# A dense layer on quarter products: sums made in the output projection, and the down product on 7 of 8 quarter products too

## The chip, the core and the metric

One core of a Trainium2 chip runs the program alone. The metric is the device time of one execution, in microseconds (us), as the median over runs. Per core there are the matrix engine (PE), the vector engine (DVE), the activation engine (ACT), GpSimd (POOL), and the sync engine (SP), which here issues loads; 16 DMA engines move data between HBM (also the kernel's own scratch tensors) and on-chip memory (SBUF). PE writes to accumulators (PSUM).

## The reference, cut to what matters

A decoder trunk of two layers on 1024 rows of width 1024, all in fp32. The change lies in the first layer's second half and at its borders:

```python
def swiglu(h, w_gate, w_up, w_down):
    return (jax.nn.silu(h @ w_gate) * (h @ w_up)) @ w_down
...
h = h + retnet_gla_mixer(hn, positions, ab_w_in[e], ..., ab_w_out[e])
h = h + swiglu(rms_norm(h, norm_ffn_g[l]), ffn_w_gate[e], ffn_w_up[e], ffn_w_down[e])
```

The hidden width is 2816 = 22 tiles of 128. The second layer (an HGRN2 mixer, then routed experts) follows.

## The kernel before, in words

**Three matmuls for one.** Each fp32 operand is held as two fp32r numbers, hi and lo; `mm3` (L154 to L156) does hi x hi, lo x hi and hi x lo. ACT makes hi by a copy and DVE makes lo by a subtraction: `whi`, `wlo` for weights (L142, L143, or `split_to`, L817, L818), `xhi`, `xlo` for activations. Two raw weight tiles ("wst") and four split ones fit in the weight pool.

**Order.** The program is written as one stream; a scheduler of the framework gives each engine its own list, and every engine works through its list in order. An instruction that waits holds all behind it on its engine, also a load on SP or a store on POOL. `defer` puts off a piece of work by some `tick`s of the program. A tile from a pool with n buffers waits until the last reader of the tile n allocations ago is done.

**Output projection** (`outproj`, `outproj_ab`). For each of 8 row tiles: load h, two accumulations of 24 matmuls, two adds on DVE (L765), then store h to scratch, norm to hn (ACT L192, POOL L182 and L184, DVE L194), and by `rows_to_fm` turn hn with 8 transposes on PE (L204) into the two halves of x (`xhi`, `xlo`: 8 blocks of features by 512 rows).

**Gate and up** (`gate_up_quads`). The two products gate and up are taken as one 2x2 block product: rows in two halves, features in two halves, and [gate, up] as two columns. Seven products of quarters (Winograd's form of Strassen's scheme) replace eight. `quad_sums` makes four sums of quarters of x on DVE (L833, L838), and splits them, while the first tile runs. For each f of 22, `quad_weights` loads the gate and up weights of one tile (512 KB each, into "raw", 8 buffers), makes four sums on DVE (L880 to L883) and splits all; then seven products of 12 matmuls follow in accumulators A, B, C and Dk, with copies on ACT (p1, p5, d, u2) and adds on DVE between. The sixth product adds to C, so it waits for C's copy p5 (L914). Two 256 KB stores of hid per f go through POOL's queue (L922, L928).

**Down** (`ffn_down`). Row tiles in groups of 3, 3 and 2. For each group, hid is read from scratch two f tiles at a time (L956) and split, w_down is loaded whole, and 1056 matmuls in all add up over 22 tiles; then h is added (L973), stored, normed and turned for the next mixer, `mix_c`.

Of the kernel before, what the change touches and what calls it, by code (L numbers as in the profile page):

```python
# [18 lines left out]
T = 1024  # L19
# [21 lines left out]
FFN_TILES = ((0, 3), (3, 3), (6, 2))  # L41
# [33 lines left out]
class Trunk:  # L75
# [142 lines left out]
    def build(self, upto=9):  # L218
        nc, tc = self.nc, self.tc
        with ExitStack() as ctx:  # L220
# [8 lines left out]
            with self.pool("hnp") as self.hnp:  # L229
# [3 lines left out]
                with self.pool("op") as self.op, self.pool("w2") as w2:  # L233
                    x = self.outproj_ab(oT, (w2, 0, 4))
                if upto < 2:
                    return
                pc = self.ffn(x)
# [511 lines left out]
    def outproj(self, w, src, oT, w2, pairs, done):  # L749
# [8 lines left out]
        for t in range(8):  # L758
            h = self.t(self.op, [P, D], "h", 6)
# [9 lines left out]
    def outproj_ab(self, oT, w2):  # L769

        nc = self.nc
        g = self.gain_rows(self.op, "gain", self.i["norm_ffn_g"][0])
        x = [None, None]

        def place(hn, t):
            if t % 4 == 0:
                x[t // 4] = self.half()
            self.rows_to_fm(self.dn, hn, x[t // 4], t % 4)

        def done(h, t):  # L780
            nc.gpsimd.dma_start(self.s["h0"][t * P:(t + 1) * P, :], h)
            hn = self.norm_rows(self.op, "hn", h, g)

            self.defer(max(1, 4 * (t // 4) + 3 - t), place, hn, t)

        self.outproj(self.i["ab_w_out"][0], self.i["x"][0], oT, w2, (0, 2, 3, 1), done)
        self.flush()
        return x
# [21 lines left out]
    def ffn(self, x):  # L810

        with self.pool("ffs") as fs:
            self.gate_up_quads(fs, x)
        return self.ffn_down(x)

    def split_to(self, hi, lo, src):
        self.nc.scalar.activation(hi, src, AF.Copy)  # L817
        self.nc.vector.tensor_tensor(lo, src, hi.bitcast(F32), op=OP.subtract)  # L818

    def quad_sums(self, fs, x):  # L820


        tt = self.nc.vector.tensor_tensor
        quarter = [[[a[:, 4 * c:4 * c + 4, :] for a in x[r]] for c in range(2)] for r in range(2)]

        def tiles():
            return [self.t(fs, [P, 2, HT], "raw", 8) for _ in range(2)]

        def whole(q):
            out = tiles()  # L830
            for n, o in enumerate(out):
                hi, lo = (a[:, 2 * n:2 * n + 2, :].bitcast(F32) for a in q)
                tt(o, hi, lo, op=OP.add)  # L833
            return out

        def sums(dst, a, b, op):
            for o, p, q in zip(dst, a, b):
                tt(o, p, q, op=op)  # L838
            return dst

        def split(src, name):
            s = [self.t(fs, [P, 4, HT], name + n, 1, F32R) for n in ("hi", "lo")]
            for n, r in enumerate(src):
                self.split_to(*(a[:, 2 * n:2 * n + 2, :] for a in s), r)
            return s
# [673 lines left out]
```

## Time and profile before

| | us |
|---|---|
| median of three runs | 4001.97 (4001.89 to 4003.94) |
| profiled execution, its own time | 4004.72 |
| its span in the trace | 4003.0 |
| gate/up: first to last matmul | 566.62 to 1006.58 |
| down: first to last matmul | 1022.01 to 1270.61 |

A row of the timeline gives start, length, engine, line, operation, result <- operands, a count, and in brackets how long the engine had been idle and what it had waited for. Matmul rows overlap: a 128x512 one has 0.39 us, but at full clock the next starts 0.23 later, so spacing is what counts. PEclk is the granted clock of PE as a share of the higher of its two levels, 2.4 GHz; 0.5 is the lower, 1.2 GHz.

### The profile page before, as it was taken

The page shows a single profiled execution, that of the slowest core. Times are in us where ns is not written, and L with a number is a line of the kernel's source. Part 1 is how long each engine was busy: PE and PEld are TensorE (multiplying, and loading weights), DVE is VectorE, ACT ScalarE, POOL GpSimd, SP SyncE. Part 2 cuts the span into 40 slices and gives each one's busy share as a digit, 9 for nine tenths or more (in the row PEclk, how much of TensorE's full clock was granted, in tenths as well). Part 3 has the DMA queues.
Part 4 walks back from the last instruction along what each step waited for, and adds up shares of the span by engine and source line. Part 5 has one row for each costly group of instructions (what it writes and reads, how often), then busy time and mean ns, then how long its engine had stood idle before and what let it go on. Part 6 is the DMA issues. An engine that isn't in the chain of part 4 may idle for free. (4 is left out here: it accounts for less than half of the span.)

```text
span 4003.0 us, 63918 instructions
## 1 busy us (share of the span) xinstructions
PE 3886.5 (97%) x26096; PEld 3600.8 (90%) x26096; DVE 2037.9 (51%) x2974; ACT 1500.0 (37%) x2311; POOL 278.6 (7%) x418
## 2 busy tenths in 40 slices
PE   8999989999899999999799999999999999999998
PEld 7888868888688889998798999999999999999996
DVE  5743356554355363354554544544545545455564
ACT  4212323333344222222344444444434444444453
POOL 1011000000001000003100000000000000000012
PEclk9999989999999999999899999999999999999999
DMA  4011313221665111113466555555555555566686
GB/s 133 27 48 61 127 51 99 82 82 63 193 201 182 43 33 53 43 64 123 161 192 201 165 175 176 164 160 192 183 171 179 184 184 182 189 190 201 211 287 223
DMA packets 436559, 568.17 MB, mean 142 GB/s; under 512 B 25734, under 2 KB 340390, under 8 KB 436256
## 3 DMA queue, kind: packets, MB, share of 16 engines
q1 hardware_dynamic: 415120, 493.87, 38.5%
q0 software_dynamic: 21136, 70.13, 5.0%
q8 instruction: 206, 3.38, 0.4%
q14 instruction: 97, 0.79, 0.1%
HBM read 511.11 MB, written 51.87 MB: 141 GB/s over the span
## 5 line engine op out<-in xcount | busy, mean ns | idle before, releaser
L143 DVE TENSOR_TENSOR wlo<-wst,whi 128x1024 fp32r<-128x1024 f32 (+1 forms) x816 | 995.7, 1223 | 1285.4 <-ACT whi L142 1272.3
L142 ACT ACTIVATE whi<-wst 128x1024 fp32r<-128x1024 f32 (+1 forms) x816 | 859.5, 1056 | 1097.9 <-PE pj L155 588.0
L155 PE MATMUL pj<-mxl,whi 128*128 128x256 f32 (+5 forms) x3584 | 1028.7, 287 | 0.2 <-DVE mxl L1242 0.2
L156 PE MATMUL pj<-mxh,wlo 128*128 128x256 f32 (+5 forms) x3584 | 1028.2, 287 | 0.0
L154 PE MATMUL pj<-mxh,whi 128*128 128x256 f32 (+5 forms) x3584 | 1026.9, 287 | 0.1
L154 PEld LDWEIGHTS pj<-mxh,whi 128*128 128x128 f32 x3584 | 675.5, 188 | 0.7 <-ACT sl L1259 0.3
L155 PEld LDWEIGHTS pj<-mxl,whi 128*128 128x128 f32 x3584 | 675.2, 188 | 0.5 <-DVE mxl L1242 0.4
L156 PEld LDWEIGHTS pj<-mxh,wlo 128*128 128x128 f32 x3584 | 673.4, 188 | 0.0
L154 PE MATMUL pj<-whi,xhi 128*128 128x256 f32 (+2 forms) x1280 | 400.9, 314 | 6.0 <-DVE h L973 4.0
L155 PE MATMUL pj<-wlo,xhi 128*128 128x256 f32 (+2 forms) x1280 | 398.9, 312 | 0.3 <-DVE wlo L143 0.3
L156 PE MATMUL pj<-whi,xlo 128*128 128x256 f32 (+2 forms) x1280 | 398.9, 312 | 0.0
L154 PE MATMUL dn<-mhh,whi 128*128 128x288 f32 (+4 forms) x1120 | 326.2, 291 | 0.0
L155 PE MATMUL dn<-mhl,whi 128*128 128x288 f32 (+4 forms) x1120 | 325.3, 290 | 0.0
L156 PE MATMUL dn<-mhh,wlo 128*128 128x288 f32 (+4 forms) x1120 | 325.1, 290 | 0.0
L154 PEld LDWEIGHTS pj<-whi,xhi 128*128 128x128 f32 x1280 | 248.8, 195 | 18.6 <-issue 4.8
L155 PEld LDWEIGHTS pj<-wlo,xhi 128*128 128x128 f32 x1280 | 249.4, 195 | 9.9 <-DVE wlo L143 1.0
L156 PEld LDWEIGHTS pj<-whi,xlo 128*128 128x128 f32 x1280 | 249.1, 195 | 9.3
L154 PE MATMUL pj<-xhi,whi 128*128 128x512 f32 x624 | 246.2, 395 | 5.4 <-ACT whi L817 3.5
L156 PE MATMUL pj<-xhi,wlo 128*128 128x512 f32 x624 | 245.5, 393 | 0.1
L155 PE MATMUL pj<-xlo,whi 128*128 128x512 f32 x624 | 244.8, 392 | 0.0
L155 PEld LDWEIGHTS dn<-mhl,whi 128*128 128x128 f32 x1120 | 210.9, 188 | 0.0
L156 PEld LDWEIGHTS dn<-mhh,wlo 128*128 128x128 f32 x1120 | 210.7, 188 | 0.0
(359 smaller groups left out, 5449.8 us busy)
## 6 DMA issues: line engine op xcount, KB each, us to landing
wst<-in_moe_w_gate_dram SPq DMA_DIRECT2D x224, 512.0 KB, 3.8
wst<-in_moe_w_up_dram SPq DMA_DIRECT2D x224, 512.0 KB, 3.9
wst<-in_moe_w_down_dram SPq DMA_DIRECT2D x224, 512.0 KB, 4.4
wst<-in_ffn_w_down_dram SPq DMA_DIRECT2D x66, 512.0 KB, 3.6
wst<-in_c_w_in_dram SPq DMA_DIRECT2D x32, 512.0 KB, 3.7
wst<-in_ab_w_in_dram SPq DMA_DIRECT2D x26, 512.0 KB, 3.8
scr_h<-h POOLq DMA_DIRECT2D x24, 512.0 KB, 3.4
raw<-in_ffn_w_gate_dram SPq DMA_DIRECT2D x22, 512.0 KB, 3.8
```

Source lines behind the costliest of these rows:

```text
L142: act = nc.scalar.activation(hi, st, AF.Copy)
L143: dve = nc.vector.tensor_tensor(lo, st, hi.bitcast(F32), op=OP.subtract)
L154: mm(ps, l[0], r[0], start=start, stop=False, **kw)
L155: mm(ps, l[0], r[1], start=False, stop=False, **kw)
L156: self.last_mm = mm(ps, l[1], r[0], start=False, stop=stop, **kw)
```

## The change

The turned quarters of x and their four sums are no longer made from xhi and xlo in front of gate/up, but from rows of hn in the output projection: hn of row tiles 0 to 3 is stored to scratch, and for tiles 4 to 7 the matching tile of the upper half is loaded again (`ht`), three sums of rows are made on POOL (on DVE for the last tile), and everything is turned by `turn`. The fourth sum is kept as rows in scratch (`s3r`) and turned at the start of gate/up. The f tiles are taken in pairs (j, j + 11), third and fourth product change places. After each pair POOL makes four sums of its hid blocks and stores seven blocks, and four sums of w_down's quarters (1 MB, `wd`, one buffer), stored to scratch `wt`. The down product then is seven quarter products of 132 matmuls over all rows, 924 in all, accumulated into h; h is loaded up front.

```diff
-    def quad_sums(self, fs, x):
...
+    def turn(self, rows, dst, t):
+        ps = self.dn([P, 4, P])
+        for k in range(4):
+            self.nc.tensor.transpose(ps[:, k, :], rows[:, k * P:(k + 1) * P], self.ident)
+        self.split_to(*(a[:, :, t * P:(t + 1) * P] for a in dst), ps)
...
         def done(h, t):
             nc.gpsimd.dma_start(self.s["h0"][t * P:(t + 1) * P, :], h)
             hn = self.norm_rows(self.op, "hn", h, g)
+            if t < 4:
+                nc.gpsimd.dma_start(self.s["hn0"][t * P:(t + 1) * P, :], hn)
+                self.defer(1, place, hn, t)
+                return
+            ht = self.t(self.op, [P, D], "ht", 1)
+            r = slice((t - 4) * P, (t - 3) * P)
+            nc.sync.dma_start(ht, self.s["hn0"][r, :])
+            s1 = h[:, L]
+            tt = (nc.vector if t == 7 else nc.gpsimd).tensor_tensor
+            tt(s1, hn[:, L], hn[:, R], op=OP.add)
+            tt(hn[:, L], ht[:, L], hn[:, L], op=OP.subtract)
+            tt(ht[:, L], s1, ht[:, L], op=OP.subtract)
+            tt(ht[:, R], ht[:, R], ht[:, L], op=OP.subtract)
+            nc.gpsimd.dma_start(self.s["s3r"][r, :], hn[:, L])
+            self.defer(1, place2, hn, t - 4, ht, s1)
...
-        g, u = (self.t(fs, [P, 2, 4, P], "raw", 8) for _ in range(2))
+        g, u = (self.t(wp, [P, 2, 4, P], "wst", 2) for _ in range(2))
...
-        ta, tb = (self.t(fs, [P, 2, 4, P], "raw", 8) for _ in range(2))
+        ta, tb = (self.t(fs, [P, 2, 4, P], "raw", 4) for _ in range(2))
...
+            for f in [a * NH + j for j in range(NH) for a in range(2)]:
+                W = self.quad_weights(fs, wg, wu, f * P)
+                if f == 0:
+                    for t in range(4):
+                        r = sn()
+                        nc.sync.dma_start(r, self.s["s3r"][t * P:(t + 1) * P, :])
+                        self.turn(r, X[6], t)
...
+                    self.keep("hid", 3, j, a22)
+                    pt(s1, a21, a22, op=OP.add)
+                    self.keep("hid", 4, j, s1)
+                    pt(a21, a11, a21, op=OP.subtract)
...
+                    b = self.t(fs, [P, 2, 2, HT], "wd", 1)
+                    nc.sync.dma_start(b, wd.rearrange("(r p) (c n) -> p r c n", p=P, c=2)[:, j::NH])
+                    pt(b[:, 0, 0], b[:, 0, 1], b[:, 0, 0], op=OP.subtract)
+                    pt(b[:, 0, 1], b[:, 1, 1], b[:, 0, 1], op=OP.subtract)
+                    pt(b[:, 1, 1], b[:, 1, 1], b[:, 0, 0], op=OP.subtract)
+                    pt(b[:, 1, 0], b[:, 1, 1], b[:, 1, 0], op=OP.subtract)
+                    for n, a in enumerate((b[:, 0, 0], b[:, 1, 1], b[:, 0, 1], b[:, 1, 0])):
+                        self.keep("wt", n, j, a)
...
+        W = [wd[:, :NH, :HT], wd[:, NH:, :HT], wd[:, NH:, HT:], wt[3], wt[0], wt[1], wt[2]]
...
+            hs = [self.t(fp, [P, D], "h", 8) for _ in range(8)]
+            for t, h in enumerate(hs):
+                nc.sync.dma_start(h, self.s["h0"][t * P:(t + 1) * P, :])
...
+            def product(n, ps, first=True, last=True):
...
+                    own = n or j0
+                    for dst, src, pool in ((l, hv[n], fp if own else None), (r, W[n], None)):
+                        wp = self.wps[0][0]
+                        st = self.t(pool or wp, [P, 2, HT], "wst", 4 if pool else 2)[:, :nj]
+                        nc.sync.dma_start(st, src[:, js])
+                        dst += [self.t(pool or wp, [P, 2, HT], a, 3 if pool else 4, F32R)[:, :nj] for a in ("whi", "wlo")]
+                        self.split_to(*dst, st)
+                    for j in range(nj):
+                        for u in range(4):
+                            self.mm3(ps[u], [a[:, j, u * P:(u + 1) * P] for a in l], [a[:, j, :] for a in r],
+                                     first and j0 + j == 0, j0 + j == NH - 1, **kw)
...
+            product(2, B, False)
+            add(0, 1, B)
+            for t in range(4):
+                self.defer(1 + t, finish, t)
+            A = [self.pj([P, HT]) for _ in range(4)]
+            product(3, A)
+            pc = self.piece(i["c_w_in"][0], 2048)
+            self.flush()
+            add(1, 0, A, OP.subtract)
+            for t in range(4, 8):
+                finish(t)
```

The change moves instructions in three places. PE, at the end of the output projection, before: from its last matmul to the first of gate/up (pj600).

```order
L156 MATMUL pj556_4608<-whi503_4092,xlo435_3806 128x512
L204 MATMUL dn562_4644<-ident_64,hn545_4511 128x128 x4
L204 MATMUL dn563_4651<-ident_64,hn545_4511 128x128 x4
L204 MATMUL dn564_4658<-ident_64,hn551_4573 128x128 x4
L204 MATMUL dn565_4665<-ident_64,hn551_4573 128x128 x4
L204 MATMUL dn566_4672<-ident_64,hn557_4635 128x128 x4
L204 MATMUL dn567_4679<-ident_64,hn557_4635 128x128 x4
L204 MATMUL dn571_4694<-ident_64,hn568_4687 128x128 x4
L204 MATMUL dn572_4701<-ident_64,hn568_4687 128x128 x4
L154 MATMUL pj600_4785<-xhi529_4390,whi578_4719 128x512
L155 MATMUL pj600_4785<-xlo530_4391,whi578_4719 128x512
L156 MATMUL pj600_4785<-xhi529_4390,wlo579_4720 128x512
```
And after, from the last turn of row tile 6 on (pj609, the first product, with 12 matmuls, stands just ahead; hn578, h563 and ht581 are row tile 7, sn601 to sn607 the four s3r rows; dn610 is the second product):

```order
L782 MATMUL dn577_4749<-ident_64,ht573_4721 128x128 x4
L782 MATMUL dn582_4771<-ident_64,hn578_4757 128x128 x4
L782 MATMUL dn583_4778<-ident_64,h563_4631 128x128 x4
L782 MATMUL dn584_4785<-ident_64,ht581_4764 128x128 x4
L782 MATMUL dn585_4792<-ident_64,ht581_4764 128x128 x4
L782 MATMUL dn602_4834<-ident_64,sn601_4832 128x128 x4
L782 MATMUL dn604_4843<-ident_64,sn603_4841 128x128 x4
L782 MATMUL dn606_4852<-ident_64,sn605_4850 128x128 x4
L153 MATMUL pj611_4870<-s0hi479_4043,whi595_4820 128x512
L154 MATMUL pj611_4870<-s0lo480_4044,whi595_4820 128x512
L782 MATMUL dn608_4861<-ident_64,sn607_4859 128x128 x4
L153 MATMUL dn610_4869<-xhi432_3803,whi593_4812 128x512
```
Transposes of tiles that come from scratch (ht, sn) now stand among the first matmuls of gate/up, and the second product stands behind the last of them.

SP, in the first f tiles of gate/up, before (574 and 575 are the weights of the first f tile, and so on):

```order
L868 DMA raw574_4713<-in_ffn_w_gate_dram 128x8x128
L868 DMA raw575_4714<-in_ffn_w_up_dram 128x8x128
L868 DMA raw608_4891<-in_ffn_w_gate_dram 128x8x128
L868 DMA raw609_4892<-in_ffn_w_up_dram 128x8x128
L868 DMA raw628_5023<-in_ffn_w_gate_dram 128x8x128
L868 DMA raw629_5024<-in_ffn_w_up_dram 128x8x128
L868 DMA raw648_5155<-in_ffn_w_gate_dram 128x8x128
L868 DMA raw649_5156<-in_ffn_w_up_dram 128x8x128
```
And after, from behind the loads of s3r (617 and 618 are the second f tile's):

```order
L938 DMA wd638_5114<-in_ffn_w_down_dram 128x2x1024
L852 DMA wst617_4972<-in_ffn_w_gate_dram 128x8x128
L852 DMA wst618_4973<-in_ffn_w_up_dram 128x8x128
L852 DMA wst639_5124<-in_ffn_w_gate_dram 128x8x128
L938 DMA wd680_5396<-in_ffn_w_down_dram 128x2x1024
L852 DMA wst640_5125<-in_ffn_w_up_dram 128x8x128
L938 DMA wd722_5678<-in_ffn_w_down_dram 128x2x1024
L852 DMA wst659_5254<-in_ffn_w_gate_dram 128x8x128
L938 DMA wd764_5960<-in_ffn_w_down_dram 128x2x1024
L852 DMA wst660_5255<-in_ffn_w_up_dram 128x8x128
L852 DMA wst681_5406<-in_ffn_w_gate_dram 128x8x128
L938 DMA wd806_6242<-in_ffn_w_down_dram 128x2x1024
```
Between the weights of the f tiles now stand the loads of w_down's quarters, three for two f tiles; there are eleven.

ACT, in the middle of an f tile, before (sn646 is p5, the copy of accumulator C, pj642; raw648 and raw650 are weights and a sum of weights of the f tile after):

```order
L817 ACTIVATE whi652_5161<-raw648_5155 128x1024
L912 ACTIVATE sn644_5053<-sn644_5053 128x512
L914 ACTIVATE sn646_5055<-pj642_5051 128x512
L817 ACTIVATE whi654_5169<-raw650_5159 128x1024
L916 ACTIVATE sn645_5054<-dn643_5052 128x512
L918 ACTIVATE sn647_5056<-pj640_5049 128x512
```
And after (sn657 is p5, the copy of C, pj653; wst659 and raw661 belong to the f tile after):

```order
L775 ACTIVATE whi663_5260<-wst659_5254 128x1024
L903 ACTIVATE sn655_5154<-sn655_5154 128x512
L905 ACTIVATE sn656_5155<-dn654_5153 128x512
L775 ACTIVATE whi665_5268<-raw661_5258 128x1024
L907 ACTIVATE sn657_5156<-pj653_5152 128x512
L909 ACTIVATE sn658_5157<-pj651_5150 128x512
```
The split of the next f tile's first sum (raw661, made on DVE from its gate and up weights) has moved from behind p5 to ahead of it.

SP, at the border to the down product, before:

```order
L132 DMA wst1060_7795<-in_ffn_w_down_dram 128x1024
L132 DMA wst1063_7819<-in_ffn_w_down_dram 128x1024
L214 DMA gain1029_7667<-in_norm_mix_g_dram 128x1024
L951 DMA h1030_7669<-scr_h0 128x1024
L951 DMA h1031_7671<-scr_h0 128x1024
L951 DMA h1032_7673<-scr_h0 128x1024
L956 DMA hid1039_7681<-scr_hid 128x2x384
L956 DMA hid1048_7735<-scr_hid 128x2x384
L956 DMA hid1057_7789<-scr_hid 128x2x384
```
And after (wst1073, the hid rows of the first two tiles of the first product, was loaded before these; wst1079 are those of the next two):

```order
L986 DMA wst1106_8157<-in_ffn_w_down_dram 128x512
L986 DMA wst1116_8189<-in_ffn_w_down_dram 128x2x512
L213 DMA gain1060_7949<-in_norm_mix_g_dram 128x1024
L966 DMA h1061_7951<-scr_h0 128x1024
L966 DMA h1062_7952<-scr_h0 128x1024
L966 DMA h1063_7953<-scr_h0 128x1024
L966 DMA h1064_7954<-scr_h0 128x1024
L966 DMA h1065_7955<-scr_h0 128x1024
L966 DMA h1066_7956<-scr_h0 128x1024
L966 DMA h1067_7957<-scr_h0 128x1024
L966 DMA h1068_7958<-scr_h0 128x1024
L986 DMA wst1079_8007<-scr_hid 128x2x512
```
Eight loads of h now stand where three stood, and the second load of hid stands behind all of them.

## Rows read from the trace of the kernel before

**Rows 1.** The page's first part: busy time, share of the span, instructions.

```profile
PE 3886.5 (97%) x26096; PEld 3600.8 (90%) x26096; DVE 2037.9 (51%) x2974; ACT 1500.0 (37%) x2311; POOL 278.6 (7%) x418
```
**Rows 2.** Windows: busy time of each engine with its count of instructions, then granted clock of PE, share of DMA time, GB/s. Two parts of gate/up, the middle of the stop behind it, and down.

```profile
566.60:612.00 45.40, 34.76 (x108) 24.62 (x108) 41.76 (x44) 16.39 (x20) 1.16 (x2) 0.80 0.19 58
612.00:1008.00 396.00, 394.73 (x1740) 326.53 (x1740) 219.76 (x290) 153.67 (x212) 22.16 (x41) 1.00 0.25 81
1014.00:1022.00 8.00, 0.00 (x0) 0.00 (x0) 0.01 (x1) 0.84 (x1) 0.00 (x0) 0.50 1.02 396
1030.00:1270.00 240.00, 239.83 (x1081) 198.26 (x1080) 122.93 (x124) 99.18 (x118) 13.18 (x18) 1.00 0.61 194
```
**Rows 3.** Timeline, the end of the output projection and the start of gate/up.

```profile
555.28 0.40 PE L156 MATMUL pj<-whi,xlo 128*128 128x512 f32 x1
555.52 3.27 PE L204 MATMUL dn<-ident,hn 128*128 128x128 f32 x24
555.72 0.69 DVE L765 TENSOR_TENSOR h<-h,pj 128x512 f32<-128x512 f32 x1 [4.76 <-PE pj L156]
561.63 1.94 PE L204 MATMUL dn<-ident,hn 128*128 128x128 f32 x8 [2.84 <-DVE hn L194]
566.62 0.80 PE L154 MATMUL pj<-xhi,whi 128*128 128x512 f32 x1 [3.06 <-ACT whi L817]
```
**Rows 4.** Timeline, the last matmuls of gate/up and the start of down.

```profile
1004.54 0.39 PE L156 MATMUL pj<-s3hi,wlo 128*128 128x512 f32 x1
...
1006.58 0.39 PE L156 MATMUL pj<-s3hi,wlo 128*128 128x512 f32 x1
1009.34 0.68 DVE L927 TENSOR_TENSOR sn<-sn,sn 128x512 f32<-128x512 f32 x1
1010.31 1.62 SPq L951 DMA_DIRECT2D h<-scr_h  x3
1012.02 1.78 SPq L956 DMA_DIRECT2D hid<-scr_hid  x3
1021.12 0.84 ACT L817 ACTIVATE hh<-hid 128x768 fp32r<-128x768 f32 x1 [12.76 <-DMA hid<-scr_hid]
1022.01 0.79 PE L154 MATMUL pj<-whi,hh 128*128 128x512 f32 x1 [15.04 <-ACT hh L817]
```
**Rows 5.** Timeline, matmuls of down after that stop.

```profile
1026.58 0.63 PE L155 MATMUL pj<-wlo,hh 128*128 128x512 f32 x1
1027.01 0.63 PE L156 MATMUL pj<-whi,hl 128*128 128x512 f32 x1
...
1028.29 0.44 PE L156 MATMUL dn<-whi,hl 128*128 128x512 f32 x1
1028.57 0.39 PE L154 MATMUL dn<-whi,hh 128*128 128x512 f32 x1
```
**Rows 6.** Groups of instructions by line and shape, 540 to 1280 us: shape, count, busy us, mean ns of one, idle time before them.

```profile
L818 DVE TENSOR_TENSOR wlo<-raw,whi 128x1024 fp32r<-128x1024 f32 x66 | 80.5, 1223 | 86.5 <-ACT whi L817 86.5
L817 ACT ACTIVATE whi<-raw 128x1024 fp32r<-128x1024 f32 x66 | 69.7, 1060 | 116.7 <-PE dn L155 74.1 <-PE pj L155 35.2 <-PE pj L156 4.5
L881 DVE TENSOR_TENSOR raw<-raw,raw 128x512 f32<-128x512 f32 x22 | 15.0, 684 | 0.0
L914 ACT ACTIVATE sn<-pj 128x512 f32<-128x512 f32 x22 | 13.2, 598 | 33.0 <-PE pj L156 33.0
L922 POOL DMA_DIRECT2D scr_hid<-sn x22 | 12.0, 544 | 349.2 <-DVE sn L921 349.2
```
**Rows 7.** DMA issues: count, KB each, median us from issue to landing.

```profile
raw<-in_ffn_w_gate_dram SPq DMA_DIRECT2D x22, 512.0 KB, 3.8
wst<-in_ffn_w_down_dram SPq DMA_DIRECT2D x66, 512.0 KB, 3.6
scr_hid<-sn POOLq DMA_DIRECT2D x44, 256.0 KB, 2.3
hid<-scr_hid SPq DMA_DIRECT2D x11, 256.0 KB, 3.6
```
**Rows 8.** POOL beside DVE: a group by line, then the timeline at three places far from the change.

```profile
L623 POOL TENSOR_TENSOR qq<-qq,t 128x512 f32<-128x512 f32 x8 | 12.4, 1549 | 20.5 <-DVE t L622 20.2
L623 POOL TENSOR_TENSOR qk<-qk,t 128x512 f32<-128x512 f32 x8 | 10.2, 1279 | 31.2 <-DVE t L622 30.9
260.56 1.23 DVE L143 TENSOR_TENSOR wlo<-wst,whi 128x1024 fp32r<-128x1024 f32 x1
260.61 2.33 POOL L623 TENSOR_TENSOR qq<-qq,t 128x512 f32<-128x512 f32 x1 [0.83 <-DVE t L622]
18.34 1.27 DVE L194 SCALAR_TENSOR_TENSOR s<-qk,rstd,vg 128x1024 f32<-128x1024 f32 x1
29.27 0.66 POOL L289 CAST mk<-row 128x576 uint8<-128x576 f32 x1
29.35 1.66 DVE L194 SCALAR_TENSOR_TENSOR s<-qk,rstd,vg 128x1024 f32<-128x1024 f32 x1 [0.29 <-POOL rstd L184]
```
**Rows 9.** Timeline, the end of down and the first matmul of mix_c.

```profile
1270.61 0.39 PE L156 MATMUL pj<-whi,hl 128*128 128x512 f32 x1
1275.03 0.55 PE L154 MATMUL pj<-whi,xhi 128*128 128x256 f32 x1 [4.03 <-DVE h L973]
```

More of the change, by code (lines that the diff above doesn't have):

```diff
@@ L40 @@
 EPS = 1e-6
-FFN_TILES = ((0, 3), (3, 3), (6, 2))
 LEVELS = (1, 2, 4, 8, 16, 32, 64)
@@ L232, in build @@
                     oT = self.mix_ab(x)
[L233 to L237, printed above, removed]
+                x = [None, None]
+                with self.pool("fs") as fs:
+                    X = [[self.t(fs, [P, 4, HT], f"s{n}{a}", 1, F32R) for a in ("hi", "lo")] for n in range(2)]
+                    with self.pool("op") as self.op, self.pool("w2") as w2:
+                        self.outproj_ab(oT, (w2, 0, 4), X)
+                    if upto < 2:
+                        return
+                    q = [[[a[:, 4 * c:4 * c + 4, :] for a in oT[r]] for c in range(2)] for r in range(2)]
+                    self.ffn_gate_up([q[0][0], q[0][1], q[1][0], q[1][1], X[0], X[1], None])
+                pc = self.ffn_down(x)
                 if upto < 3:
@@ L746, in mix_c, with outproj @@
         return oT
-    def outproj(self, w, src, oT, w2, pairs, done):
+    def outproj(self, w, src, oT, w2, pairs, done, nh=6):
         nc = self.nc
@@ new lines, in product @@
+            def product(n, ps, first=True, last=True):
+                kw = {} if first else dict(skip_group_check=True)
+                for j0 in range(0, NH, 2):
+                    nj = min(2, NH - j0)
+                    js = slice(j0, j0 + nj)
+                    l, r = [], []
+                    own = n or j0
+                    for dst, src, pool in ((l, hv[n], fp if own else None), (r, W[n], None)):
+                        wp = self.wps[0][0]
+                        st = self.t(pool or wp, [P, 2, HT], "wst", 4 if pool else 2)[:, :nj]
[6 more added lines that the diff above has]
+                                     first and j0 + j == 0, j0 + j == NH - 1, **kw)
+                    self.tick()
@@ new lines, in add @@
+            def add(r, c, ps, op=OP.add):
+                for u in range(4):
+                    hc = hs[4 * r + u][:, c * HT:(c + 1) * HT]
+                    tt(hc, hc, ps[u], op=op)
+            A = [self.pj([P, HT]) for _ in range(4)]
+            product(0, A)
+            add(0, 0, A)
+            B = [self.dn([P, HT]) for _ in range(4)]
+            product(1, B)
+            add(0, 0, B)
+            product(5, A, False)
+            add(0, 1, A)
+            B = [self.dn([P, HT]) for _ in range(4)]
@@ L976, in ffn_down @@
+            product(4, B)
+            add(1, 1, B)
+            product(6, A, False)
+            add(1, 0, A)
+            add(1, 1, A)
+            product(2, B, False)
+            add(0, 1, B)
+            for t in range(4):
+                self.defer(1 + t, finish, t)
+            A = [self.pj([P, HT]) for _ in range(4)]
+            product(3, A)
+            pc = self.piece(i["c_w_in"][0], 2048)
             self.flush()
+            add(1, 0, A, OP.subtract)
+            for t in range(4, 8):
+                finish(t)
```

189 lines of the change are left out of this document (72 added, 117 removed).

## The prediction

> **What bounds the kernel now.** I read the page's first part (PE busy 97% of the span [rows 1]: time is saved only by giving PE less, or by closing a stop), then the windows over the dense layer [rows 2], then the timeline at its three borders [rows 3, 4, 9]. In 612 to 1008 us PE is busy 394.73 of 396 us at full clock, and DVE, ACT and DMA have room: PE's matmuls set that stage. Before it, in 566.6 to 612, PE has 34.76 of 45.4 us at a mean clock of 0.80. Behind it lies a stop of 15 us, which ends on the load of hid [rows 4], and behind the second product one of 4 us [rows 9]. One 128x512 matmul costs (1006.58 - 1004.54) / 9 = 0.2267 us. All offsets below count from the last output-projection add, 555.72 [rows 3]. Gate/up ends at 1006.81, which is +451.1; its 22 x 7 x 12 = 1848 matmuls need 418.9, so 21.3 of its 440.2 us are stops and half clock, nearly all ahead of 612.
>
> **Output projection.** Four rows of sums are turned there too: 16 more transposes at 3.27/24 = 0.136 us [rows 3], **+2.2**. The loads of hn, its stores and POOL's sums lie beside its matmuls, until the last tile.
>
> **The front of gate/up.** The sums on DVE and the 11.3 us between the last output-projection matmul and the first of gate/up go. What is late next is a chain through DRAM: PE runs in order, and the turns of the last two tiles and of the s3r rows stand ahead of the second product. There is one ht buffer. Its tile for t=5 is turned by +2; load 3.8 [rows 7]; three POOL sums that need it, 1.28 each [rows 8]; eight transposes, +10.8; the next load 3.8, one DVE sum 0.69, POOL's issue 0.54 [rows 6] and the store's 2.3, then a 256 KB load at 3.6 [rows 7]: **+22**. By then 14 of the 1848 matmuls are done. The other 1834 take 415.8 and the restart costs 3 us of half clock (14 matmuls at 0.43 in place of 0.23, as after the stop of down [rows 5]). Without other stops gate/up ends at +440.8: **-10.3**. Bounds: 4 us either way, by the loads.
>
> **The new chain in gate/up.** The rows of w_down are summed on POOL while gate/up runs. They have one buffer, so a load waits for the four stores of the load before, and SP, in order, holds the up-weights behind it: after the fourth wd load comes the fourth tile's up-weights, and so on, three wd loads for two tiles, until the eleventh. A cycle is: the 1 MB load, 3.8 plus 512 KB more at 396 GB/s (1.33) [rows 2, 7] = 5.1; four POOL sums; four issues 4 x 0.54; the last store's 2.3. For a POOL sum the rows give 1.28 alone, 2.33 beside a DVE instruction with both inputs in SBUF; I take 1.55, the mean of the eight of qq [rows 8], since DVE is busy 219.76 of 396 us [rows 2]. Cycle: 5.1 + 6.2 + 2.2 + 2.3 = 15.8. Each pair of tiles adds its own four sums and seven stores, 6.2 + 3.8 = 10 us of POOL, about half of it under a wd load: 5. So the chain needs 3 x 15.8 + 5 = 52.4 us for what PE does in 168 x 0.2267 = 38.1.
>
> When up-weights come late this is what stops PE: DVE's sums from them stand in its order ahead of the current tile's later work, and ACT's split of the first sum stands ahead of the copy (p5) that frees C for the sixth product. First time: the first wd load is issued at +20 behind the s3r loads, the fourth at +67.4, the up-weights behind it land 6.4 later, +73.8. Then five DVE instructions (four of 0.68 and a wlo of 1.22 [rows 6], 4.0). DVE waits for POOL too: the product at 29.35 took 1.66 where its like at 18.34 took 1.27, with a POOL cast running until 29.93 [rows 8]. POOL is then in the middle of eight sums, so I let four of the five wait 1.28: 9.0; whi 1.06; copy 0.60 [rows 6]: +84.5. The third tile starts at 22 + 3 + 154 x 0.2267 = +59.9 and wants C after 60 matmuls, +73.5. Stop: 11. Twice more the chain loses 52.4 - 38.1 = 14.3. With 3 us of half clock at the last restart: **+42.6**. Behind the eleventh wd load it is over; seven more pairs have slack. Bounds, with neither engine holding the other: cycle 14.7, pair 4.5, first stop 2.6 and twice 10.5, 26.6 with the restart; below, nothing, if the cycle were under 12.7 (a third of 38.1); above, a cycle of 18, 62.
>
> In the Trainium skill, "SBUF — State Buffer", section "Who interferes with whom", a DVE instruction with two SBUF inputs and a GpSimd instruction that reads SBUF need one read port pair, which is an exclusive lock: who issues first has it to the end, and the other is fully blocked. That speaks against moving these sums to POOL. At 260.61 the trace agrees to the tenth: POOL starts 0.05 after DVE's 1.23 and takes 2.33, that is 1.15 from DVE's end on [rows 8]; the other way round the row at 29.35 bears it out for 0.4 us. By the rule both holds are charged (42.6); without it, 26.6.
>
> **The second product.** 7 products of 11 x 4 x 3 matmuls, 132 fewer than before: 924 x 0.2267 = 209.5. It starts at once, since its first hid rows were stored long before: the wait on hid [rows 4] goes. But only 24 matmuls have operands. SP is held by weight loads for splits that wait for those matmuls, to about 9 us behind the border; then a weight load, gain, eight h loads and the second hid load, 11 x 512 KB at 396 GB/s = 14.6, 2.4 to land, a split: 27 us behind the border, a stop of 27 - 5.4 = 22. Restart 3, 32 transposes 4.4, and mix_c follows without the 4 us stop, since its first rows are done in the last product. 238.9 against 1275.03 - 1006.81 = 268.2: **-29.3** (-24 to -38, by whether SP is held less or the loads move at fewer GB/s). Turning the last 16 more blocks in mix_c: **+2.2**.
>
> **Sum.** 2.2 - 10.3 + 42.6 - 29.3 + 2.2 = +7.4 on the profiled 4004.72, 4012.1. That execution stands 2.75 above the median 4001.97, so I forecast 4010.
>
> **Rivals.** (1) DVE and POOL hardly hold each other: 26.6 in place of 42.6, 3993. For it: POOL's 0.54 issues don't stretch beside a busy DVE, and most pairs of such instructions may miss each other. Against it: the two rows that were drawn out [rows 8]. (2) The chain keeps up and only the gains are left: faster. It decides from a cycle of 12.7 us; for that the 1 MB load and the stores must land in 5 us together, or POOL's sums run in half their 1.28. 2.2 - 10.3 - 29.3 + 2.2 = -35: 3967. Against it: three of its four terms have rows, each near its least. (3) A cycle of 18, because its own traffic slows it (two tiles' weights 2.1 MB, three wd loads and their stores 6.3, seven hid stores 1.8: 10.2 MB in 52 us, 195 GB/s where 81 moved before [rows 2]): fourth wd at +74, first stop 17.7, twice 21, 62.5 with the restart: 4029. For it: while much moves, hid landed 9 us behind its issue [rows 4].
>
> **How the numbers follow.** Forecast 0.42, rival 1 0.26, rival 2 0.1, rival 3 0.18, worse 0.04. About 8 us (0.2%) tell a change from none: faster is below 3994, so rival 2, half of rival 1 and a little more, 0.27; same, to 4010, the other half and a part of the forecast, 0.29; slower the rest, 0.44. The range 3982 to 4034 leaves out rival 2, what is beyond rival 3 and a part of it. The forecast's own range is 4000 to 4020.
>
> **What will show it.** Front: PE's first long run of matmuls starts 22 us behind the last add, released by transposes of s3r rows. Chain: three or four stops of PE in the sixth product of a tile within 60 to 200 us, ended by ACT's whi or p5, with SP waiting on wd; tile spacing 19 us afterwards. POOL's wd sums: mean 1.5 and above, some 2.3 (1.28 throughout: rival 1); DVE's 0.68 sums drawn out to 1.9. Down: 24 matmuls, then some 22 us idle, ended by DMA of hid. If all tiles keep 19 us from the first, rival 2 holds; if the stops go on past 200 us, rival 3.

## The result, and the profile after

The changed kernel takes 4032.78 us (median of four, 4028.63 to 4037.11) where the kernel before takes 4001.93 (4001.03 to 4003.94): a ratio of 1.0080, 95% interval 1.0068 to 1.0092. It is slower by 31 us; 8 were forecast, and the measured time lies near the upper end of the stated range, 3982 to 4034. The profiled execution took 4032.56, its span is 4030.7.

By stages, each from the two traces (offsets from the last output-projection add, 555.72 before and 557.68 after):

| | before | after | difference | forecast |
|---|---|---|---|---|
| last output-projection add | 555.72 | 557.68 | +2.0 | +2.2 |
| last gate/up matmul ends | +451.1 | +494.9 | +43.8 | -10.3 + 42.6 |
| from there to mix_c's first matmul | 268.2 | 241.2 | -27.0 | -29.3 |
| from there to the end of the span | 2728.0 | 2736.9 | +8.9 | +2.2 |

The down product gives what 132 matmuls fewer and two shorter borders can give. Gate/up takes it back and more. First the windows that answer to [rows 2]: four stretches of gate/up, and its border to the down product.

```profile
557.00:582.00 25.00, 13.98 (x71) 11.20 (x69) 15.41 (x36) 8.92 (x17) 8.79 (x12) 0.68 0.43 140
582.00:634.00 52.00, 51.38 (x223) 42.58 (x223) 32.18 (x36) 20.71 (x29) 29.07 (x33) 0.96 0.66 221
634.00:790.00 156.00, 125.52 (x516) 101.50 (x516) 96.05 (x90) 44.96 (x63) 88.23 (x100) 0.89 0.56 186
790.00:1052.00 262.00, 253.81 (x1107) 208.04 (x1106) 154.19 (x181) 95.46 (x131) 55.56 (x67) 0.99 0.30 98
1052.00:1084.00 32.00, 6.67 (x29) 5.27 (x28) 9.11 (x9) 5.08 (x6) 8.55 (x10) 0.64 0.83 304
```
The columns are those of [rows 2]. From 634 to 790 PE is busy 125.52 of 156 us at a mean granted clock of 0.89 (the lower level, 1.2 of 2.4 GHz, appears behind each of its three long stops), and POOL, which had 22 us of work in the 396 us of [rows 2], has 88 in this stretch alone. Even behind 790, where [rows 2] have 394.73 of 396, PE lacks 8 of 262. What it waits for, summed over gate/up and the border (the view of waits, PE's rows: us in total, times, longest):

```profile
PE pj L153 <- ACT sn L907: 38.7, 11, 11.2
PE pj L153 <- ACT whi L775: 25.3, 1, 25.3
```
L907 is the copy p5, which the sixth product of an f tile needs: eleven waits, 38.7 us. The first of them in the timeline (start, duration, engine, line and what it does, and in brackets the idle time before it and what ended that):

```profile
626.69 0.37 SPq L938 DMA_DIRECT2D wd<-in_ffn_w_down_dram  x1
627.17 0.47 SPq L852 DMA_DIRECT2D wst<-in_ffn_w_up_dram  x1
...
633.97 1.29 POOL L933 TENSOR_TENSOR sn<-sn,sn 128x512 f32<-128x512 f32 x1
634.45 5.58 DVE L864 TENSOR_TENSOR raw<-wst,wst 128x512 f32<-128x512 f32 x1 [7.17 <-DMA wst<-in_ffn_w_up_dram]
635.20 1.26 POOL L940 TENSOR_TENSOR wd<-wd 128x512 f32<-128x512 f32 x1
636.41 0.56 POOL L950 DMA_DIRECT2D scr_hid<-sn  x1
636.99 1.27 POOL L935 TENSOR_TENSOR sn<-sn,sn 128x512 f32<-128x512 f32 x1
638.21 1.26 POOL L941 TENSOR_TENSOR wd<-wd 128x512 f32<-128x512 f32 x1
...
639.95 2.40 DVE L776 TENSOR_TENSOR wlo<-wst,whi 128x1024 fp32r<-128x1024 f32 x1
639.99 1.27 POOL L942 TENSOR_TENSOR wd<-wd 128x512 f32<-128x512 f32 x1
641.20 2.16 POOL L950 DMA_DIRECT2D scr_wt<-wd  x4
642.28 0.68 DVE L865 TENSOR_TENSOR raw<-wst,raw 128x512 f32<-128x512 f32 x1
...
643.49 0.68 DVE L866 TENSOR_TENSOR raw<-raw,wst 128x512 f32<-128x512 f32 x1
...
644.28 1.06 ACT L775 ACTIVATE whi<-raw 128x1024 fp32r<-128x1024 f32 x1 [14.43 <-DVE raw L866]
645.24 0.58 ACT L907 ACTIVATE sn<-pj 128x512 f32<-128x512 f32 x1
...
645.87 0.79 PE L153 MATMUL pj<-xhi,whi 128*128 128x512 f32 x1 [11.22 <-ACT sn L907]
646.46 0.63 PE L154 MATMUL pj<-xlo,whi 128*128 128x512 f32 x1
```
The up-weights leave SP behind the 1 MB wd load, and 7.3 us later, at 634.45, DVE starts the first sum, which had waited for them. It takes 5.58 us where [rows 6] have 0.68: it ends 0.56 behind POOL's sum of 638.21. The next (wlo, 2.40 in place of 1.22) ends 1.09 behind the sum of 639.99. Then everything follows at once: the last three sums, in 0.68 each while POOL only issues stores, ACT's split, p5 (the copy of 645.24), and PE, whose matmuls take 0.79 and 0.63 at half clock in place of 0.39. From the fifth pair of f tiles on no sums of w_down are left (the last ends at 760), and it looks like this, once in each pair:

```profile
900.19 1.30 POOL L931 TENSOR_TENSOR sn<-sn,sn 128x512 f32<-128x512 f32 x1
900.49 1.57 DVE L864 TENSOR_TENSOR raw<-wst,wst 128x512 f32<-128x512 f32 x1 [3.33 <-DMA wst<-in_ffn_w_up_dram]
...
902.37 1.31 POOL L933 TENSOR_TENSOR sn<-sn,sn 128x512 f32<-128x512 f32 x1
902.58 2.19 DVE L776 TENSOR_TENSOR wlo<-wst,whi 128x1024 fp32r<-128x1024 f32 x1
...
904.56 1.36 POOL L935 TENSOR_TENSOR sn<-sn,sn 128x512 f32<-128x512 f32 x1
904.70 1.78 DVE L865 TENSOR_TENSOR raw<-wst,raw 128x512 f32<-128x512 f32 x1
...
908.76 0.58 ACT L907 ACTIVATE sn<-pj 128x512 f32<-128x512 f32 x1
...
909.39 0.50 PE L153 MATMUL pj<-xhi,whi 128*128 128x512 f32 x1 [1.16 <-ACT sn L907]
```
Three DVE instructions (1.57, 2.19 and 1.78; alone 0.68, 1.22 and 0.68) are drawn out by one sum of hid each, everything behind them is late, and PE stops 1.5 us, from 907.85 on (2.8 in one of these seven pairs). The front, which answers to [rows 3]:

```profile
567.17 1.12 PE L782 MATMUL dn<-ident,ht 128*128 128x128 f32 x4 [3.63 <-POOL ht L818]
...
575.42 1.94 PE L782 MATMUL dn<-ident,ht 128*128 128x128 f32 x8 [3.55 <-DVE ht L818]
...
580.16 1.94 PE L782 MATMUL dn<-ident,sn 128*128 128x128 f32 x8 [2.80 <-DMA sn<-scr_s3r]
...
582.72 1.09 PE L782 MATMUL dn<-ident,sn 128*128 128x128 f32 x4 [0.62 <-DVE s3lo L776]
583.46 0.78 PE L153 MATMUL pj<-s0hi,whi 128*128 128x512 f32 x1
```
The turns of tiles from scratch and of s3r come in four steps with stops between, and the run of matmuls begins at 583.5, 25.8 behind the add. The border, answering to [rows 4] (the first 24 matmuls of down run from 1052.61 to 1058):

```profile
1064.67 5.48 SPq L966 DMA_DIRECT2D h<-scr_h  x8
1071.63 13.47 SPq L986 DMA_DIRECT2D wst<-scr_hid  x5
1082.43 1.06 ACT L775 ACTIVATE whi<-wst 128x1024 fp32r<-128x1024 f32 x1 [22.00 <-DMA wst<-scr_hid]
...
1083.54 0.79 PE L153 MATMUL pj<-whi,whi 128*128 128x512 f32 x1 [25.33 <-ACT whi L775]
```
Eight h loads are issued from 1064.67 on, the second hid load at 1071.63, and its split starts at 1082.43. Last, groups by line, 560 to 1060 us, answering to [rows 6 and 8]: two of POOL's sums, one of w_down and one of hid, and four groups of DVE's.

```profile
L942 POOL TENSOR_TENSOR wd<-wd 128x512 f32<-128x512 f32 x11 | 15.5, 1413 | 0.2
L929 POOL TENSOR_TENSOR sn<-sn,sn 128x512 f32<-128x512 f32 x11 | 14.3, 1302 | 0.2
L864 DVE TENSOR_TENSOR raw<-wst,wst 128x512 f32<-128x512 f32 x22 | 31.0, 1409 | 73.0 <-DMA wst<-in_ffn_w_up_dram 73.0
L865 DVE TENSOR_TENSOR raw<-wst,raw 128x512 f32<-128x512 f32 x22 | 25.1, 1139 | 0.0
L776 DVE TENSOR_TENSOR wlo<-wst,whi 128x1024 fp32r<-128x1024 f32 x26 | 40.9, 1575 | 8.0 <-ACT whi L775 8.0
L911 DVE TENSOR_TENSOR sn<-sn,pj 128x512 f32<-128x512 f32 x22 | 15.1, 688 | 70.2 <-PE pj L155 70.2
```
POOL's eight sums of a pair take 1.29 to 1.41 on average, hardly more than alone. DVE's of L864, L865 and L776 took 0.69, 0.68 and 1.22 before and now average 1.41, 1.14 and 1.58; L911, which has one operand in an accumulator, takes 0.69 as before. Taken one by one, the 128x512 sums on DVE in gate/up fall into two kinds. With both operands in SBUF (L864 to L867, L912, L917), the 29 that overlapped a POOL sum by more than 0.3 us took 0.97 to 5.58, and the others at most 0.70. With one operand in an accumulator (L902, L911, L914, L916), the 18 that overlapped one took 0.67 to 0.69.

### The profile page after: what moved, and what is told of

The parts are those of the page before. It is cut to its first block, busy times and chain, and to the rows that moved or that the text cites. A ratio compares the mean times of both kernels' runs of the same rounds, so it can differ in the third digit from the quotient of the medians.

```text
span 4030.7 us, 64021 instructions
## 1 busy us (share of the span) xinstructions
PE 3862.8 (96%) x26012; PEld 3581.5 (89%) x26012; DVE 2069.4 (51%) x2967; ACT 1483.6 (37%) x2300; POOL 458.6 (11%) x603
## 3 DMA queue, kind: packets, MB, share of 16 engines
q0 software_dynamic: 28192, 93.47, 6.5%
## 5 line engine op out<-in xcount | busy, mean ns | idle before, releaser
L142 DVE TENSOR_TENSOR wlo<-wst,whi 128x1024 fp32r<-128x1024 f32 (+1 forms) x750 | 914.6, 1222 | 1211.1 <-ACT whi L141 1194.2
L141 ACT ACTIVATE whi<-wst 128x1024 fp32r<-128x1024 f32 (+1 forms) x750 | 789.7, 1056 | 1012.7 <-PE pj L154 576.2
L153 PE MATMUL pj<-xhi,whi 128*128 128x512 f32 x624 | 249.5, 400 | 39.3 <-ACT sn L907 38.7
L154 PEld LDWEIGHTS pj<-wlo,xhi 128*128 128x128 f32 x1280 | 247.2, 193 | 10.3 <-DVE wlo L142 1.4
```

The costliest lines, as they stand in the source:

```text
L141: act = nc.scalar.activation(hi, st, AF.Copy)
L142: dve = nc.vector.tensor_tensor(lo, st, hi.bitcast(F32), op=OP.subtract)
L153: mm(ps, l[0], r[0], start=start, stop=False, **kw)
L154: mm(ps, l[0], r[1], start=False, stop=False, **kw)
```

## The experiments

Theory A (queue): up-weights come late behind one-buffer wd loads on SP. Theory B (hold): DVE's instructions with both operands in SBUF are held by POOL's sums. Theory C: the traffic slows the loads. Theory D (buffers): the change also cut the buffers of the up-weights, and with them the slack in which a held DVE would cost nothing. The median of the kernel before was 3996 to 3999 in the later sessions, so I compare ratios to it, and stages from the traces by their offsets from the last output-projection add. "Stops" are gaps of PE ahead of a sixth product, counted from the start of one matmul to the start of the next (0.23 us of each is the usual spacing). A diff without another mark is against the changed kernel.

**The wd load on POOL's queue.**

```diff
-                    nc.sync.dma_start(b, wd.rearrange(...)[:, j::NH])
+                    nc.gpsimd.dma_start(b, wd.rearrange(...)[:, j::NH])
```

> Edit: the loads of w_down's quarters go through POOL's queue in place of SP's; sums and stores as they were. Theory A (queue): PE's three stops of 11.6, 9.4 and 9.1 us in the sixth product come from up-weights that stand behind one-buffer wd loads on SP; the hold of DVE by POOL's sums only lengthens each by some 5 us. Then no stop of 9 us is left; what stays are stops of 2 to 5 us where DVE is held, and gate/up is 8 to 20 us shorter: 4012 to 4025. Theory B (hold): the stops come from DVE's sums being held by POOL, the queue is innocent. Then three stops of about 9 us or more stay and the time is within 4028 to 4037. Theory C (traffic): loads are slow because 195 GB/s move; nothing changes in what moves, so stops and time stay as in B.

Ratio 1.0034 (1.0021 to 1.0046). Gate/up ends at +491.5, 3.4 earlier; stops of 8.3, 4.9, 8.8 and 3.3 us remain, at other tiles, then the 1.5 us ones. The end of the program took 17.0 us in place of 24.2 (below). The runs of this kernel spread from 4003 to 4021, and the profiled one is the slowest, 10.6 above the median; even if all of that lay in gate/up, the queue would be worth some 14 us of the 43.8. By time alone B's expectation was a miss and A's was not: this kernel stands 15 us over the kernel before, the changed one 31. But 7.2 of these 16 us lie at the end of the program, and A is too small: with SP free, most of the loss in gate/up is still there.

**w_down's sums on DVE.**

```diff
-                    pt(b[:, 0, 0], b[:, 0, 1], b[:, 0, 0], op=OP.subtract)
+                    tt(b[:, 0, 0], b[:, 0, 1], b[:, 0, 0], op=OP.subtract)
...
```

> Edit: the four sums of w_down's quarters on DVE (0.69 us each) in place of POOL; load, buffer and queue as they were. The cycle of a wd load falls from about 15 to 5.1 + 4 x 0.7 + 2.2 + 2.4 = 12.5, under the 12.7 that PE leaves it, and nothing of w_down holds DVE any more. A and B both: the three stops fall to under 2 us each, gate/up is 30 to 38 us shorter, 3993 to 4003; the 1.5 us stops at the end of each pair stay, since the sums of hid are still POOL's. C: the same bytes move in the same time, so stops of 7 us or more stay, over 4022.

Ratio 1.0015 (1.0004 to 1.0025). Gate/up ends at +470.1, 24.8 earlier; the longest stop is 3.1. Two of three wd loads follow the one before in 11.0 to 11.7 us, every third in 19.8 to 20.9 (in the changed kernel mostly 14.8 to 16.8, and 18.9 to 19.9), so this takes away the hold by these sums and the late loads together. It speaks against C, since the same bytes moved and the loads came faster.

**One wd load per pair, sums still on POOL.** The load is issued behind the pair's second up-weights (`last_ld` is the last load of gate or up weights).

```diff
+                    with self.tc.issue_after(self.last_ld.ins):
-                    nc.sync.dma_start(b, wd.rearrange(...)[:, j::NH])
+                        nc.sync.dma_start(b, wd.rearrange(...)[:, j::NH])
```

> Edit: each wd load is ordered on SP behind the up-weights of the second f tile of its pair, one load per pair in place of three per two tiles; POOL keeps all its sums. A: no up-weights wait for a wd load that waits for stores, so no stop above 5 us; but at each of the eleven pairs POOL's sums meet DVE's, stops of about 2.4 us, some 24 us in all with little half clock: gate/up 10 to 22 us shorter, 4010 to 4023. B: the stops of 9 us and more stay or spread over all pairs: 4028 or above. C: the traffic is thinned to 160 GB/s, the stops go as in A.

Ratio 1.0077 (1.0053 to 1.0101), gate/up ends at +499.7, 4.8 later. No stop exceeds 4.2 us, but there are nine of 4.2. A's expectation of 10 to 22 us was a miss: thinning out the loads spreads the hold over all pairs.

**The same, with w_down's sums on DVE.** Both diffs above together.

> Edit: e3_pace (one wd load per pair, behind the up-weights) with w_down's four sums on DVE; hid's sums stay on POOL. Load, queue, buffer and order of loads are those of e3_pace, where PE stopped 4.2 us at ten pairs and gate/up ended at 500. B (hold): the stops fall to the 1.5 us that hid's sums cost, gate/up ends at 458 to 465. If the paced load itself made them (the up-weights behind a 1 MB load on SP), they stay at 4 us and gate/up ends above 485.

Ratio 0.9982 (0.9973 to 0.9992), a little faster than before. Gate/up ends at +457.2 (458 to 465 expected; the run above has nine stops of 4.2, not ten). Order, queue, buffer and pace of the loads are those of the run above; only the engine of four sums differs. PE's wait for p5 in the two runs, the paced one first:

```profile
PE pj L153 <- ACT sn L907: 35.3, 11, 3.8
```
```profile
PE pj L153 <- ACT sn L907: 10.4, 9, 1.2
```
DVE's fourth and fifth instruction of an f tile whose up-weights have landed, again the paced run first:

```profile
630.79 2.27 DVE L867 TENSOR_TENSOR raw<-wst 128x512 f32<-128x512 f32 x1
631.20 1.30 POOL L940 TENSOR_TENSOR wd<-wd 128x512 f32<-128x512 f32 x1
632.58 1.60 POOL L941 TENSOR_TENSOR wd<-wd 128x512 f32<-128x512 f32 x1
632.98 1.74 DVE L866 TENSOR_TENSOR raw<-raw,wst 128x512 f32<-128x512 f32 x1
```
```profile
633.23 0.68 DVE L867 TENSOR_TENSOR raw<-wst 128x512 f32<-128x512 f32 x1
633.83 0.68 DVE L866 TENSOR_TENSOR raw<-raw,wst 128x512 f32<-128x512 f32 x1
```
35.3 us of waits against 10.4, 3.8 the longest against 1.2, and 42.5 us of gate/up (499.7 - 457.2, with the half clock behind the longer stops): at this order and pace of the loads, that is what w_down's sums cost on POOL, and the two instructions show the hold.

**hid's sums on DVE, w_down's on POOL.**

```diff
-                    pt(s1, a21, a22, op=OP.add)
+                    tt(s1, a21, a22, op=OP.add)
...
```

> Edit: of the changed kernel, only the four sums of hid per pair go to DVE; w_down's sums stay on POOL, one buffer, on SP's queue. This isolates the stops of 1.5 us and the 39.5 us pairs (in place of 38.1) that the changed kernel shows from the fourth pair on, which my prediction put at nothing. B: they are DVE held by the sums of hid; then all pairs behind the third take 38.1 again and gate/up ends 10 to 14 us earlier for that alone, 3 to 8 more since the first three pairs' POOL work is shorter: 470 to 482 in place of 495, with three stops of 6 to 11 us left. Rival: the 1.5 us come from DVE's own order or from buffers of hid; then they stay, gate/up ends above 487.

Ratio 1.0042 (1.0029 to 1.0054). Behind the fourth pair every pair takes 38.1 us and no stop of 1.5 us is left: those were the hold by hid's sums. The three stops, though, grew to 13.0, 12.0 and 10.6 (DVE has more to do in front of them), so gate/up ends at +485.8, 4 above the range that I gave.

**Six buffers for the up-weights.**

```diff
-        g, u = (self.t(wp, [P, 2, 4, P], "wst", 2) for _ in range(2))
+        g, u = (self.t(fs, [P, 2, 4, P], "raw", 6) if c else self.t(wp, [P, 2, 4, P], "wst", 2) for _ in range(2))
...
-        ta, tb = (self.t(fs, [P, 2, 4, P], "raw", 4) for _ in range(2))
+        ta, tb = (self.t(fs, [P, 2, 4, P], "raw", 6) for _ in range(2))
```

> Edit: gate and up weights of all f tiles but the first go to the raw pool with six buffers in place of two wst buffers; sums stay on POOL, wd load on SP with one buffer. Theory D (buffers): up-weights land only 6 us after a tile starts because their one buffer is freed by the last split of the tile before, so there is no slack for a DVE held by POOL; with six buffers they land one tile earlier, the 1.5 us stops at the end of the pairs go, and the three stops fall under 6 us each: gate/up ends at 460 to 478 in place of 495, time 15 to 30 us under the changed kernel's. B alone: DVE's sums are drawn out as before and PE stops 9 us three times, gate/up ends above 485.

Ratio 1.0023 (1.0013 to 1.0033). Here gate and up weights and their sums share one ring of six buffers, in place of two and four. Gate/up ends at +466.9, 28 earlier, with all sums on POOL; the 1.5 us stops are gone and one of the three, but two of 8.3 and 7.5 stay. So with room in front of them, held DVE instructions cost nothing in the later pairs: D holds there, and only in part for the three stops. Those two end in another instruction, DVE's wlo:

```profile
PE dn L155 <- DVE wlo L776: 15.0, 2, 7.9
PE pj L153 <- ACT sn L907: 2.0, 3, 0.8
```

**h loads behind the first hid loads.**

```diff
-            for t, h in enumerate(hs):
-                nc.sync.dma_start(h, self.s["h0"][t * P:(t + 1) * P, :])
+            def load(r):
+                with self.tc.issue_after(self.last_ld.ins):
+                    for t in range(4 * r, 4 * r + 4):
+                        nc.sync.dma_start(hs[t], self.s["h0"][t * P:(t + 1) * P, :])
...
             product(0, A)
+            load(0)
...
             product(4, B)
+            load(1)
```

> Edit: the eight h loads of the down product are ordered on SP behind the hid and weight loads of the first product (rows 0 to 511) and of the fourth (rows 512 to 1023). My reading of the 25.7 us stop after the first 24 matmuls of down: the second hid load stands behind gain and eight h loads. Then the stop falls by 8 loads x 1.33 = 11 us to 13 to 16 us, total 4019 to 4024. Rival: hid is late by itself (its stores, or SP held by the weight loads ahead); then the stop stays above 22 us and the time within 4028 to 4037.

Ratio 1.0062 (1.0038 to 1.0086). The stop is 15.2 in place of 25.7, and down takes 230.7 in place of 241.2: the eight loads cost 10.5 us. I put the remaining 15 down to SP held by weight loads and to the hid load itself, as the prediction does; no run tests that. (`last_ld` is here the last load of an operand of the down product.)

**All of it: every sum on DVE, one load per pair, h late.** The four diffs of these parts together, those of the buffers and of POOL's queue left out.

> Edit: all eight sums of a pair (w_down's and hid's) on DVE, the wd load ordered once per pair behind the up-weights (as e3_pace), h loads late (as e4_hlate). What e1 to e3 left open: is it the hold of DVE by POOL's sums that stops PE (theory B), or DVE's lateness in itself? B: with no POOL sum left in gate/up no f tile after the first takes more than 19.2 us, gate/up ends 441 to 447 us behind the last output-projection add (before: 451), down takes 230, and the whole is 33 to 45 us under before, ratio 0.989 to 0.992. Rival: DVE has 2.7 us more per f tile pair side, 69% busy, and is late by itself: stops of 1 to 4 us at every pair stay, gate/up ends above 455, ratio above 0.993.

3962.98 us (3962.38 to 3963.98) against 3997.01, ratio 0.9914 (0.9895 to 0.9932): faster than both kernels. Gate/up ends at +443.6, every f tile from the second on takes 19.04 us, down takes 229.6. The 400 us in the middle of gate/up:

```profile
600.00:1000.00 400.00, 400.00 (x1766) 331.42 (x1765) 271.62 (x370) 154.56 (x211) 59.99 (x111) 1.00 0.47 157
```
PE is busy 400.00 of 400 us, with DVE at 68%: DVE was never short of time, only held. L864, L865 and L776 take 0.69, 0.68 and 1.22 on average again, while the same bytes move in less time: that speaks against theory C once more.

**The end of the program.** Behind its last matmul the changed kernel takes 24.2 us, before 17.4. The raw records of the trace name POOL's closing drain (10.04 us against 4.40) and the semaphore step ahead of it (2.63 against 1.26). I tried what it hangs on: one wd store in place of four (alone, and with all of the edits of the run above), and the kernel before with its hid stores split by rows or by columns.

```diff
-                    for n, a in enumerate((b[:, 0, 0], b[:, 1, 1], b[:, 0, 1], b[:, 1, 0])):
-                        self.keep("wt", n, j, a)
+                    nc.gpsimd.dma_start(self.s["wt"].rearrange(...)[:, :, j], b.rearrange("p r c n -> p (r c) n"))
```

(The down product then takes the parts of wt in their new order.) The two against the kernel before, by rows and by columns:

```diff
-            nc.gpsimd.dma_start(self.s["hid"][f * P:(f + 1) * P, :HT], p1)
+            for a, b in ((0, 48), (48, 96), (96, 128)):
+                nc.gpsimd.dma_start(self.s["hid"][f * P + a:f * P + b, :HT], p1[a:b])
...
+            for a, b in ((0, 256), (256, 512)):
+                nc.gpsimd.dma_start(self.s["hid"][f * P:(f + 1) * P, a:b], p1[:, a:b])
...
```

> Edit: the four stores of a wd block (256 KB each) are one of 1 MB: 257 DMAs on POOL's queue in place of 290 (before: 205). Two questions. The cycle: 5.1 + 5.3 + 0.6 + about 5 for a 1 MB store = 16 in place of 15, so the three stops stay, 9 to 13 us each. The end of the program: POOL's closing drain takes 4.4 us in before and in e1_wd_queue (301 DMAs), 10.04 in all the others (290). If it grows with the number of DMAs it is 7 to 8 here; if it hangs on where the queue's ring stands at the end it is again one of the two values.

> Edit: g1_best with the merged store of d1_merge. With one load per pair the cycle has 38 us, so nothing in gate/up changes against g1_best (within 2 us); the program's end shows the same drain as d1_merge.

> Edit, on the kernel before: each of the 44 hid stores on POOL's queue is split by rows in three (48, 48 and 32 rows): 293 DMAs on POOL's queue in place of 205, the same bytes and rows of 2 KB. If the closing drain (4.4 us in before, 10.04 in the changed kernel with 290) and the semaphore step ahead of it (1.26 and 2.63) hang on the number of DMAs, they are about 10 and 2.6 here and the time behind the last matmul is 24 us in place of 17.4; if on the rows moved, 4.4 and 17.4. The rest of the kernel is unchanged, within 2 us.

> Edit, on the kernel before: each of the 44 hid stores is split by columns in two (1 KB of each of 128 rows): 249 DMAs, 44 x 128 = 5632 more rows of descriptors, the same bytes. In the changed kernel 85 more DMAs brought about 10900 more rows. If rows count, the drain here lies about half way, 7 us, or at one of the two values if it is stepped; if the number of DMAs counts, near 9.7, as in d1_merge with 257.

| kernel | DMAs on POOL's queue | packets of that queue | drain, us |
|---|---|---|---|
| before | 205 | 21136 | 4.40 |
| hid stores split by columns | 249 | 21840 | 6.53 |
| hid stores split by rows | 293 | 23248 | 6.37 |
| merged wd store; with all edits | 257 | 27664 | 9.71; 9.79 |
| changed kernel, and seven others | 290 | 28192 | 10.04 |
| wd load on POOL's queue | 301 | 31184 | 4.40 |

Neither number orders the drain: it rises to 10 and is 4.40 again with most DMAs and most packets. What sets it stays open. As to time, the split stores leave the kernel before within what can be told (1.0007, 0.9997 to 1.0018, and 1.0010, 1.0000 to 1.0021), the merged store alone has ratio 1.0105 (1.0080 to 1.0130; two runs) with stops of 15.1, 13.8 and 13.7 (a longer cycle, mostly 16.6 to 18.1; the stops are above what was expected), and with all edits 0.9911 (0.9891 to 0.9931), like the run without it.

## Why the prediction was right, and where it was off

**Right: the direction, and the mechanism of the loss.** The chain was there: wd loads left SP 14.8 to 16.8 us apart, 18.9 to 19.9 where a pair's own sums lay between (forecast 15.8 and 5 more), and once 18.3 behind up-weights that waited for their buffer, the first stop was 11.6 (forecast 11), and the three pairs with long stops took 14.8, 12.2 and 10.9 us more than 38.1, 37.9 in all (forecast 42.6). But of that, I had counted 14.3 twice for stops that were 9.4 and 9.1, and half clock once, "at the last restart": it came behind each stop and cost 2.8, 3.0 and 2.0 us (what the f tiles of 33.2, 31.2 and 29.9 us have over 19.0, less the stops). Two errors that partly cancelled.

**Wrong: "Behind the eleventh wd load it is over; seven more pairs have slack".** They have none. The sums of hid hold DVE in every pair, and up-weights with one buffer land too late to give a held DVE room: 13.0 us over these pairs, 1.4 in each of six and 4.3 in one, the only one with half clock behind its stop. This is the term that was missing, and the two runs that take away the hold of hid's sums or give buffers both remove it. The diff has the buffers of the gate and up weights fall from eight, shared with their sums, to two, and the working gave them no step.

**Luck in the time.** The forecast's sum was 20 us short of the profiled difference (+7.4 against +27.7). The range reached that far only for the sake of rival 3, which did not occur; what filled it were these 13.0 us and 6.8 at the program's end, which stand in no term.

**Off in kind: which engine waits.** I let POOL wait (1.55 a sum) and DVE wait four times 1.28. POOL took 1.33 on average; DVE bore it. In the Trainium skill, "SBUF — State Buffer", section "Who interferes with whom", the lock goes to whoever issues first and the other is fully blocked. The timelines agree that DVE's wait lasts to the end of a POOL sum (two instructions of 0.68 end 0.57 and 0.56 behind the POOL sums of 900.19 and 904.56), and show something that the sentence doesn't say: a waiting DVE instruction can be passed by several POOL sums in a row. My split, 42.6 with the hold and 26.6 without, no run tests: to take a sum off POOL shortens the cycle too. What the runs show is that the eight sums on POOL cost 56.1 us at one load per pair (499.7 against 443.6), and that without them, and with the loads paced, gate/up ends 51.3 us earlier than in the changed kernel and nothing of the chain is left.

**Front, -10.3 forecast.** 443.6 against 451.1 without the chain, so -7.5. The run of matmuls began 25.8 behind the add where I had 22: the turns themselves ran at half clock (1.12 us for four, 0.54 in [rows 3]), and the s3r turns were taken in two goes.

**Down, -29.3.** -27.0. The stop was 25.7 and not 22; the cause was as forecast, and the run with late h loads shows it for 10.5 us of the stop.

**Behind it, +2.2.** +2.1 from mix_c's first matmul to the last matmul of the kernel; then 6.8 for the longer end, in no view of the profile of before and in no step of mine.

**The rivals.** Rival 1 (hardly any hold) fell with the first trace, by DVE's sums; by the sign that I had set on POOL's wd sums (1.5 and above, 1.28 for rival 1) the measured 1.33 would have pointed to it. Rival 2 (the chain keeps up) did not occur, but its condition did for two loads of three when DVE made w_down's sums: cycles of 11 us, under its 12.7, and the three long stops were gone; every third cycle still took 20, and the three pairs took 42.4 to 42.7. Rival 3 gave nearly the measured time, 4029, for a reason that wasn't there: of ten cycles four took 18 or more, three of them with a pair's own sums between, and no stop was 17.7. Its sign, stops past 200 us, was there, but those stops come from hid's sums, when all wd loads are over.

**Not shown.** The queue alone, with a cycle of 15 us and no hold, was not tried; on the changed kernel its worth is bounded only by the run with the load on POOL's queue. Once w_down's sums were on DVE, pacing the loads was worth 12.9 us (470.1 against 457.2).

## What to carry to other kernels

An idle engine is not free room: before a sum goes to POOL, look which DVE instructions with two SBUF operands stand one step ahead of the critical one, and how many microseconds of slack their operands' buffers leave; here the sums cost 56 us on POOL (499.7 against 443.6), and on DVE, at 68% load, no stop. When a stretch is emptied by fewer matmuls, check what the loads of the stretch behind it are queued behind: eight early h loads took 10.5 of the 30 us that the matmuls gave. Pacing bulk loads by an order edge paid once w_down's sums no longer held DVE (gate/up at 457.2, without it 470.1), and not before (499.7 against 494.9).

## What was not expected of the hardware

DVE instructions of 0.69 us took up to 5.58 us beside POOL (6.28 in the run with the merged store alone): one waited through four POOL sums, three of which started after it (633.97 to 639.47 in the first timeline), while POOL's sums in the same runs took 1.3 to 1.4 on average. It waited also through the half microsecond in which POOL only issued a DMA (636.46 to 636.99); why stays open, since 13 like it in the changed kernel that overlapped POOL's issues by more than 0.3 us, and no POOL sum, took at most 0.69. And the closing drain of POOL differs by 5.6 us between kernels that do the same work at the end, by a rule that the variants here did not show.
